# Where a weight matrix is split into two parts: on ScalarE and VectorE, or in two transfers of the POOL queue

## The chip, the cores and the metric

The kernel runs on one core of a Trainium2 chip. The metric is the device time of one launch in microseconds; the kernel before took 1216.84 us (median of 2 runs, 1215.64 to 1218.04). The engines are named as in the profile: PE is TensorE (matmuls; PEld is its loading of weights), DVE is VectorE, ACT is ScalarE, POOL is GpSimd, SP is the engine that only issues transfers. A transfer is issued on the queue of an engine, here SP's or POOL's, and each queue is worked through in order.

## The reference

One inference step of a one-layer decoder: 1024 prompt positions and 8 single-token decode sequences, width 1024. Four recurrent mixers (S5, SSD, HGRN2, GLA), all fed by one input projection, are followed by an output projection and an MLP. What matters here is the MLP:

```python
hn = rmsnorm(x, p['norm_mlp_g'])
x = x + jnp.square(jax.nn.relu(hn @ p['w_up'])) @ p['w_down']
```

`w_up` is 1024 x 4096 and `w_down` 4096 x 1024, all in float32. The other outputs are the recurrent states.

## The kernel before

The 1032 positions are worked on as two halves of the sequence, 512 columns (`hf` = 0) and 520 columns (`hf` = 1, in two chunks of 260). The channels lie on the 128 partitions.

**Products in two parts.** A float32 operand is held as the sum of two float32r tiles, a high part and a low part. `split` (line 213) makes them: ScalarE rounds the float32 tile into `hi` (`act`, line 157), VectorE subtracts `hi` from it into `lo` (`tt`, line 169). `mm3` (line 256) then issues three matmuls for each block of 128 x 128 weights: hi with hi, hi with lo, lo with hi, in that order. All matmuls go through line 199.

**Weights.** `wprep` (line 240) fetches one tile of 128 x 1024 weights in two halves of 512 columns: SP loads `raw` (line 249), and `split` makes `hi` and `lo`. Below, such a half of 256 KB is called a half weight. The buffers are `W_BUFS = 3, 4, 4` for `raw`, `hi` and `lo` (line 100); the projections and the MLP share them. A buffer is free again when the last instruction that reads it is done.

**Order.** `main` (line 1697) runs the input projection of both halves, the output projection and MLP of the first, then those of the second. `drive` (line 300) puts the mixers' work, two strands of their own, between the main products by estimated times. The order of the instructions on each engine and queue comes from a planner (line 1888) that simulates the program: an instruction is placed when the planner expects its operands to be there, lower priority numbers first. `wprep` runs 1000000 ahead of the rest (`Prio`).

**The MLP** (`mlp`, line 1454) has 8 blocks `fb` of 512 hidden channels. For each block of the first half it makes four products with `w_up` (`f` = 0 to 3, `product`, line 471, 8 blocks of weights each), squares the ReLU (`up`, line 1419) into four tiles `a`, and makes four products with `w_dn` (`q` = 0 to 3), each for two output blocks `n2` over the four `f`. For q = 0 the order of (n2, f) is written out at line 1489: n2 = 0 with f 0 to 2, n2 = 1 with f 0 to 2, then both with f = 3; column block `n2 * 4 + f` of the weights is used, so n2 = 0 reads the first half weight and n2 = 1 the second. Results are collected into `Y` (`collect`, line 1433).

In the second half of the sequence, block 0 runs in the same way. Blocks 1 to 7 make their up-projection in `fast_up` (line 1575) with seven products in place of eight; its weights come from `pair_weights` (line 1537), which loads `raw` on the POOL queue (line 1551) into buffers of another pool, `late`. `fast_up` also begins the down-projection of q = 0 (line 1624). Block 7 fetches its four `w_dn` tiles with `wprep` (line 1620).

**What else POOL issues.** In the output projection it stores the residual, `xd`, once for each of 8 output blocks and each half (line 1389); in the input projection it stores the projected channels (line 538).

Of the kernel before, what the change touches and what calls it, by code (L numbers as in the profile page):

```python
# [10 lines left out]
F32R = mybir.dt.float32r  # L11
I32 = mybir.dt.int32
AF = mybir.ActivationFunctionType
OP = mybir.AluOpType
# [85 lines left out]
W_BUFS = 3, 4, 4  # L100
# [7 lines left out]
class Kern:  # L108
# [131 lines left out]
    def wprep(self, src, off=-1000000, pool=None, pin=False):  # L240

        parts = []
        with Prio(self.tc, off):
            p, nr, nh, nl = (pool,) + L_BUFS if pool else (self.wp,) + W_BUFS
            for c in (slice(0, 512), slice(512, 1024)):
                raw = p.tile([128, 512], F32, tag='raw', name=self.n('raw'), bufs=nr)
                hi = p.tile([128, 512], F32R, tag='hi', name=self.n('hi'), bufs=nh)
                lo = p.tile([128, 512], F32R, tag='lo', name=self.n('lo'), bufs=nl)
                d = self.nc.sync.dma_start(raw, src[:, c])
                if pin:  # L250
                    self.tc.keep_in_program_order(d)
                self.split(hi, lo, raw)
                parts.append((hi, lo))
        return lambda k: (t[:, k % 4 * 128:k % 4 * 128 + 128] for t in parts[k // 4])

# [1198 lines left out]
    def mlp(self, hf, H2, ssq):  # L1454


        for fb in range(8):
            if hf and fb:
                A, first = yield from self.fast_up(fb, H2, R1 if fb == 7 else None)
            else:  # L1460
                A, first = [], None
                for f in range(4):
                    wt = self.wprep(self.I['w_up'][fb * 4 + f])
                    A.append(self.hidden())
                    ps = yield from self.product(hf, wt, H2)
                    if not hf and fb == f == 1:
                        R = self.inverse_squares(hf, ssq)
                    with self.first():
                        self.up(A[f], ps, hf)
                    if hf and f < 3:  # L1470
                        self.finish(8 + f)
                    if hf and f == 3:
                        ps = [self.px() for _ in CK[hf]]
                        self.sum_rows(hf, ps, ssq, True, True)
                        R1, R = self.row_factors(hf, ps), self.rows('R')
                        self.tt(R, R1, R1)
            if hf and fb == 7:
                break
            if fb == 0:
                Y = self.fp.tile([128, 8, WM], F32, tag='Y', name=self.n('Y'), bufs=1)  # L1480
                if hf:
                    self.differences(H2)
            for q in range(4):
                if q == 0 and first:
                    pp = first
                else:
                    wt, pp = self.wprep(self.I['w_dn'][fb, q]), self.pp(hf)

                    for n2, f0, f1 in ((0, 0, 3), (1, 0, 3), (0, 3, 4), (1, 3, 4)) if q == 0 else ((0, 0, 4), (1, 0, 4)):
                        yield from self.down(hf, wt, A, pp, n2, range(f0, f1))  # L1490
                with self.first():
                    for n2 in range(2):
                        self.collect(Y, q * 2 + n2, self.pieces(hf, pp[n2]), fb == 0)
                if hf and fb == 6:
                    for n2 in range(2):
                        self.residual(hf, Y, q * 2 + n2, R)
        if hf:
            yield from self.close(A, Y, self.sp.tile([128, WM], F32, tag='ssq', name=self.n('ssq'), bufs=1), first)
        else:
            self.final = Y, R, self.sp.tile([128, 512], F32, tag='nw', name=self.n('fsq'), bufs=1)  # L1500
# [74 lines left out]
    def fast_up(self, fb, H2, R):  # L1575

        h, A = 260, [self.hidden() for _ in range(4)]
        U = {}

        def step(pr, i):  # L1580
            if (pr, 'W') not in U:
                U[pr, 'W'] = self.pair_weights(fb, pr)
                U[pr, 'al'], U[pr, 'be'], U[pr, 'ga'] = self.pm()[:, :h], self.pm()[:, :h], self.px()[:, :h]
            al, be, ga = (U[pr, n] for n in ('al', 'be', 'ga'))
            bank, a, b = {1: (al, 'A11', 'B11'), 6: (be, 's2', 't2'), 7: (ga, 's3', 't3'), 2: (al, 'A12', 'B21'),
                              5: (be, 's1', 't1'), 3: (be, 's4', 'B22'), 4: (ga, 'A22', 't4')}[i]
            yield from self.seventh(U[pr, 'W'], H2, bank, a, b, i in (1, 6, 7))
            u = lambda n: self.late.tile([128, h], F32, tag=n, name=self.n(n), bufs=2)

            def out(f, c, x, bk, sign):  # L1590
                r = self.sp.tile([128, WM], F32, tag='io', name=self.n('r'), bufs=4)[:, :h]
                c0, c1 = c * h, c * h + h
                self.tt(r, bk, x, OP.add)
                if R:
                    self.stt(r, r, 0.0, R[:, c0:c1], OP.max if sign > 0 else OP.min, OP.mult)
                else:
                    self.act(r, r, AF.Relu, scale=float(sign))
                self.squares(A[f], c0, c1, r)
            f = 2 * pr
            with self.first():  # L1600
                if i == 1:
                    U[pr, 1] = u('u1')
                    self.act(U[pr, 1], al)
                elif i == 6:
                    U[pr, 2] = u('u2')
                    self.tt(U[pr, 2], be, U[pr, 1], OP.add)
                elif i == 2:
                    self.up(A[f], [(al, 0, h)], 1, R)
                elif i == 5:
                    u4 = u('u4')  # L1610
                    self.tt(u4, be, U[pr, 1], OP.add)
                    out(f + 1, 1, u4, ga, -1)
                elif i == 3:
                    out(f, 1, U[pr, 1], be, 1)
                elif i == 4:
                    out(f + 1, 0, U[pr, 2], ga, -1)
        for pr, i in ((0, 1), (0, 6), (0, 7), (0, 2), (0, 5), (1, 1), (0, 3), (1, 6), (0, 4), (1, 7), (1, 2), (1, 5)):
            yield from step(pr, i)
        if fb == 7:
            W = [self.wprep(self.I['w_dn'][7, q], pool=self.late if q > 1 else None, pin=True) for q in range(4)]  # L1620
            pp = [self.pm()[:, :h] for _ in range(2)]
            part = lambda n2, f: self.last_down(W, A, pp[n2], n2, (f,), 1)
        else:
            wt, pp = self.wprep(self.I['w_dn'][fb, 0]), self.pp(1)
            part = lambda n2, f: self.down(1, wt, A, pp, n2, (f,))
        yield from part(0, 0)
        yield from part(0, 1)
        yield from step(1, 3)
        yield from step(1, 4)
        for n2, f in ((1, 0), (1, 1), (0, 2), (1, 2), (0, 3), (1, 3)):  # L1630
            yield from part(n2, f)
        return A, (W, pp) if fb == 7 else pp
# [259 lines left out]
```

## Time and profile before

| | us |
|---|---|
| median of 2 runs | 1216.84 |
| profiled execution | 1216.4 |
| its span, first to last instruction | 1214.6 |
| PE busy | 1192.8 |
| DVE busy | 905.5 |
| ACT busy | 621.4 |
| POOL busy | 96.2 |

In the profile a group of instructions is named by its line, its engine and its tiles, out<-in; buffer numbers are left out. Where a helper issues an operation, the line is that of the helper. "Landing" of a transfer is counted from its issue. In a table by stage, each engine has its busy time and the number of its instructions, then follow the granted clock of PE, the busy share of the 16 DMA engines, and GB/s. In the list of waits stand the total, the number of times and the longest.

### The profile page before, as it was taken

To read this page: it belongs to the slowest core of one execution; us is meant where nothing else is said; L and a number is where in the kernel's file an instruction comes from. 1 tells how busy PE (TensorE), PEld (TensorE's weight loads), DVE (VectorE), ACT (ScalarE), POOL (GpSimd) and SP (SyncE) were. 2 spreads that over 40 slices of the span, in tenths; PEclk is the share of its full clock that TensorE was granted. 3 is DMA by queue.
4 is the path that set the end of the run, shared out by engine and by line. 5 is a ranking of instruction groups with operands and counts; after the bars stand their busy time and mean duration, and the time that the engine had idled before them with its cause. 6 is when DMAs were issued, how large, how long until landed. Compare 5 with 4: busy or idle time off the path is not lost. (4 is left out here: it accounts for less than half of the span.)

```text
span 1214.6 us, 23758 instructions
## 1 busy us (share of the span) xinstructions
PE 1192.8 (98%) x9107; PEld 1047.9 (86%) x9107; DVE 905.5 (75%) x2011; ACT 621.4 (51%) x1128; POOL 96.2 (8%) x159
## 2 busy tenths in 40 slices
PE   7999999999999999999999999999999999999996
PEld 4778888999988877887778787899999999999996
DVE  7997769787578589667658856496877776776896
ACT  6363353477364562555246633545675654554555
POOL 1113130000000100000000000001000100110000
PEclk9999999999999999999999999999999999999998
DMA  5564364365445352243224334356643233233432
GB/s 189 176 188 141 117 199 142 106 212 180 139 140 168 119 164 71 82 148 123 86 72 153 111 107 139 113 180 208 215 142 109 82 113 102 80 100 103 123 96 71
DMA packets 86049, 161.28 MB, mean 133 GB/s; under 512 B 13408, under 2 KB 19200, under 8 KB 85680
## 3 DMA queue, kind: packets, MB, share of 16 engines
q1 hardware_dynamic: 75952, 128.72, 33.9%
q0 software_dynamic: 9984, 31.05, 7.6%
q8 instruction: 72, 1.18, 0.4%
q14 instruction: 41, 0.34, 0.1%
HBM read 134.57 MB, written 25.16 MB: 132 GB/s over the span
## 5 line engine op out<-in xcount | busy, mean ns | idle before, releaser
L157 ACT ACTIVATE hi<-raw 128x512 fp32r<-128x512 f32 x362 | 223.7, 628 | 418.2 <-PE pm L199 327.0
L169 DVE TENSOR_TENSOR lo<-raw,hi 128x512 fp32r<-128x512 f32 x362 | 247.2, 688 | 83.4 <-ACT hi L157 82.2
L199 PE MATMUL pm<-a,hi 128*128 128x260 f32 (+1 forms) x1088 | 273.6, 338 | 0.4 <-ACT a L157 0.4
L199 PE MATMUL pm<-h,hi 128*128 128x512 f32 (+1 forms) x976 | 246.9, 344 | 0.2 <-DVE u L169 0.2
L199 PEld LDWEIGHTS pm<-a,hi 128*128 128x128 f32 x1088 | 182.8, 188 | 23.1 <-ACT a L157 0.8
L199 PEld LDWEIGHTS pm<-h,hi 128*128 128x128 f32 x976 | 164.7, 188 | 24.3 <-issue 2.0
L199 PE MATMUL pm<-a,lo 128*128 128x260 f32 (+1 forms) x544 | 171.1, 336 | 0.0
L199 PE MATMUL pm<-h,lo 128*128 128x512 f32 (+1 forms) x488 | 162.0, 343 | 0.0
L199 PE MATMUL pm<-xA,hi 128*128 128x512 f32 x352 | 114.9, 404 | 2.1 <-ACT hi L157 1.2
L199 PE MATMUL pm<-xB,hi 128*128 128x260 f32 x704 | 116.9, 287 | 0.0
L199 PEld LDWEIGHTS pm<-a,lo 128*128 128x128 f32 x544 | 97.6, 188 | 11.3 <-issue 0.3
L169 DVE TENSOR_TENSOR Y<-pm,Y 128x260 f32<-128x260 f32 (+1 forms) x120 | 63.8, 547 | 50.6 <-PE pm L199 49.9
L199 PEld LDWEIGHTS pm<-xB,hi 128*128 128x128 f32 x704 | 96.9, 188 | 3.9 <-issue 2.6
L199 PEld LDWEIGHTS pm<-h,lo 128*128 128x128 f32 x488 | 89.6, 188 | 11.4 <-issue 0.5
L199 PE MATMUL px<-a,hi 128*128 128x260 f32 x448 | 83.6, 282 | 0.0
L199 PEld LDWEIGHTS pm<-xA,hi 128*128 128x128 f32 x352 | 66.0, 190 | 20.1 <-ACT hi L157 3.9
L199 PE MATMUL pm<-xB,lo 128*128 128x260 f32 x352 | 72.4, 285 | 0.0
L199 PE MATMUL pm<-xA,lo 128*128 128x512 f32 x176 | 71.3, 405 | 0.0
L199 PEld LDWEIGHTS px<-a,hi 128*128 128x128 f32 x448 | 66.8, 188 | 0.0
L169 DVE TENSOR_TENSOR a<-r,a 128x260 fp32r<-128x260 f32 (+1 forms) x96 | 49.0, 514 | 9.1 <-ACT a L157 8.4
L199 PEld LDWEIGHTS pm<-xB,lo 128*128 128x128 f32 x352 | 54.5, 188 | 0.5
L1551 POOL DMA_DIRECT2D raw<-in_w_up_dram x56 | 30.0, 538 | 283.6 <-DVE lo L169 176.4
(435 smaller groups left out, 2030.5 us busy)
## 6 DMA issues: line engine op xcount, KB each, us to landing
raw<-in_w_dn_dram SPq DMA_DIRECT2D x128, 256.0 KB, 2.7
raw<-in_w_in_dram SPq DMA_DIRECT2D x88, 256.0 KB, 3.0
raw<-in_w_up_dram SPq DMA_DIRECT2D x72, 256.0 KB, 2.8
raw<-in_w_up_dram POOLq DMA_DIRECT2D x56, 256.0 KB, 3.0
raw<-in_w_out_dram SPq DMA_DIRECT2D x32, 256.0 KB, 3.2
x<-in_xT_dram SPq DMA_DIRECT2D x16, 260.0 KB, 3.3
x<-in_xT_dram SPq DMA_DIRECT2D x16, 256.0 KB, 3.7
xd<-x POOLq DMA_DIRECT2D x8, 260.0 KB, 3.3
```

Of the source, the lines that this page charges most:

```text
L157: return self.nc.scalar.activation(out, in_, f, **k)
L169: return self.nc.vector.tensor_tensor(out, a, b_, op)
L199: i = self.nc.tensor.matmul(out, l, r, start=start, stop=stop, **k)
L1551: self.nc.gpsimd.dma_start(x, self.I['w_up'][fb * 4 + 2 * pr + f][:, 512 * c:512 * c + 512])
```

## The change

A new function `wsplit` makes the two parts of the MLP's weights. It calls SP and VectorE no more. For each half weight POOL issues a load that converts float32 to float32r on its way into `hi`; ScalarE writes -1 times `hi` into `lo`; POOL issues a second load of the same weights that is added to `lo` as it lands. `raw` is not used there. It takes the place of `wprep` for `w_up` in `mlp` and for `w_dn` in `mlp` and in blocks 1 to 6 of `fast_up`. The input and output projections, `pair_weights` and the last block of the second half stay as they were. The numbers of buffers are the same.

```diff
+    def wsplit(self, src, off=-1000000):
+        parts = []
+        with Prio(self.tc, off):
+            for c in (slice(0, 512), slice(512, 1024)):
+                hi = self.wp.tile([128, 512], F32R, tag='hi', name=self.n('hi'), bufs=W_BUFS[1])
+                lo = self.wp.tile([128, 512], F32R, tag='lo', name=self.n('lo'), bufs=W_BUFS[2])
+                self.nc.gpsimd.dma_start(hi, src[:, c])
+                self.act(lo, hi, AF.Copy, scale=-1.0)
+                self.nc.gpsimd.dma_start(lo, src[:, c], accum_op=OP.add)
+                parts.append((hi, lo))
+        return lambda k: (t[:, k % 4 * 128:k % 4 * 128 + 128] for t in parts[k // 4])
...
-                    wt = self.wprep(self.I['w_up'][fb * 4 + f])
+                    wt = self.wsplit(self.I['w_up'][fb * 4 + f])
...
-                    wt, pp = self.wprep(self.I['w_dn'][fb, q]), self.pp(hf)
+                    wt, pp = self.wsplit(self.I['w_dn'][fb, q]), self.pp(hf)
...
-            wt, pp = self.wprep(self.I['w_dn'][fb, 0]), self.pp(1)
+            wt, pp = self.wsplit(self.I['w_dn'][fb, 0]), self.pp(1)
```

## The prediction

> **What bounds the kernel now.** I read the page first, then busy time by stage, then who waited for whom, then the groups and transfers that the change touches.
>
> ```profile
> span 1214.6 us, 23758 instructions
> PE 1192.8 (98%) x9107; PEld 1047.9 (86%) x9107; DVE 905.5 (75%) x2011; ACT 621.4 (51%) x1128; POOL 96.2 (8%) x159
> ```
>
> TensorE is busy for 98% of the span, VectorE for 75%, ScalarE for 51%. All idle time of TensorE together is 1214.6 - 1192.8 = 21.8 us. The page gives shares over the whole span, so I cut it by stage: the MLP of the first half (383 to 803 us), the output projection of the second half, the first MLP block of the second half, and its next six blocks.
>
> ```profile
> core 0: us, PE busy (x) PEld busy (x) DVE busy (x) ACT busy (x) POOL busy (x), PEclk, DMA share, GB/s
> 383.00:803.00 420.00, 417.70 (x2691) 331.73 (x2690) 291.09 (x592) 197.52 (x339) 7.79 (x5) 1.00 0.36 114
> 803.00:850.00 47.00, 47.00 (x396) 46.91 (x395) 34.70 (x62) 24.50 (x39) 5.92 (x11) 1.00 0.66 213
> 850.00:898.00 48.00, 48.00 (x394) 47.40 (x393) 39.20 (x76) 34.82 (x81) 2.15 (x4) 1.00 0.63 204
> 898.00:1160.00 262.00, 261.77 (x2177) 260.87 (x2176) 194.48 (x401) 137.45 (x294) 25.68 (x48) 1.00 0.33 104
> ```
>
> In the three stages whose weights change, TensorE idles 420.00 - 417.70 = 2.3, 0 and 0.23 us, at a granted clock of 1.00. A busy row could still hide a slow TensorE, so I look at the pace of its matmuls in the timeline and at the number of matmuls with a low part.
>
> ```profile
> 487.18 0.62 PE L199 MATMUL pm<-a,hi 128*128 128x512 f32 x2
> 487.87 0.62 PE L199 MATMUL pm<-a,hi 128*128 128x512 f32 x2
> 1068.09 2.87 PE px L199 x24
> 383.00:803.00 420.00, 202.43 (x512) 96.15 (x512) 87.14 (x128) 1.00 0.36 114
> ```
>
> The first two rows are one triple (hi, hi, lo) apart: 0.69 us for three matmuls of 512 columns, 0.23 each. The third is 24 matmuls of 260 columns in 2.87 us, 0.12 each. The last counts instructions with a low part between 383 and 803 us: 512 matmuls, and 128 on VectorE, so 128 half weights of four column blocks. A half is 12 matmuls there, 12 x 0.2315 = 2.78 us, and all are 128 x 2.78 = 355.6 of the 420 us; the rest is the mixers' small matmuls, put between. So a half comes due every 2.78 us where TensorE does nothing else, every 420 / 128 = 3.28 us on average, and every 24 x 0.12 = 2.88 us in the second half of the sequence. TensorE runs without gaps at its pace: it is the bound, and only a late operand can change the time.
>
> **What goes.**
>
> ```profile
> raw<-in_w_dn_dram SPq DMA_DIRECT2D x128, 256.0 KB, 2.7
> raw<-in_w_up_dram SPq DMA_DIRECT2D x72, 256.0 KB, 2.8
> L157 ACT ACTIVATE hi<-raw 128x512 fp32r<-128x512 f32 x362 | 223.7, 628 | 418.2 <-PE pm L199 327.0
> L169 DVE TENSOR_TENSOR lo<-raw,hi 128x512 fp32r<-128x512 f32 x362 | 247.2, 688 | 83.4 <-ACT hi L157 82.2
> ```
>
> 72 + 120 = 192 half weights take the new path: all of `w_up` that the SP queue loads, and `w_dn` without the 8 halves of the last block. VectorE loses 192 x 0.688 = 132 us. ScalarE swaps a rounding copy for a negating one of the same size, 0.63 us, so nothing. SP loses 192 issues. TensorE waits for VectorE almost nowhere (the 2.3 us above are its whole idle time in the long stage), so the gain is at most 2.3 + 0.23 = 2.5 us. I take 0.
>
> **What moves into the turnaround of a buffer.** `raw`, `hi` and `lo` have 3, 4 and 4 buffers. Before, the transfer filled a `raw` buffer ahead of time; once TensorE released a `hi` buffer, only a copy and a subtraction (0.63 + 0.69 us) stood between that and the next half. The first group shows it: ScalarE idled 327.0 us in front of this copy, waiting for TensorE's release. After, both transfers, one behind the other, and the copy lie between release and next use. The terms:
>
> ```profile
> raw<-in_w_up_dram POOLq DMA_DIRECT2D x56, 256.0 KB, 3.0
> raw<-in_w_out_dram SPq DMA_DIRECT2D x32, 256.0 KB, 3.2
> E<-cd SPq DMA_DIRECT2D x2, 1024.0 KB, 4.8
> q1 hardware_dynamic: 75952, 128.72, 33.9%
> L1551 POOL DMA_DIRECT2D raw<-in_w_up_dram x56: 537/537/544, 845.1 to 1161.4; - x56
> DMA to landing us min/median/max: 2.5/3.0/5.7
> ```
>
> Engines' share first: q1 moved 128.72 MB in 33.9% of 1214.6 us, 3.2 us per MB, so 0.84 us of all 16 engines per 0.262 MB half. One more transfer for each of 128 halves adds 128 x 0.84 / 420 = 0.26 to the share of 0.36: 0.62, about that of the output projection (0.66), whose loads land in 3.2 us where `w_dn` takes 2.7. So 0.5 us more than in a quiet stage.
>
> - Converted load: no row shows one. Bounds 2.5 and 5.7 us, the ends of the plain POOL load of the same size. I take its median and the contention, 3.0 + 0.5 = 3.5.
> - Negating copy: 0.63.
> - Adding transfer: no row shows one either. It reads the destination besides the source, so I treat it as one more 256 KB: from 2.7 us for 256 KB to 4.8 for 1 MB is 0.7 per 256 KB, so 3.5 + 0.7 = 4.2. Bounds again 2.5 and 5.7.
> - Hand-overs: release to POOL, landing to ScalarE, copy to POOL, each with what is queued ahead. POOL issues for 0.54 us and ScalarE is about half busy with instructions of 0.4 to 0.7. I take 3 x 0.4 = 1.2; bounds 0.3 and 2.5.
>
> Together 3.5 + 0.63 + 4.2 + 1.2 = 9.5 us (bounds 5.9 and 14.5).
>
> The Trainium skill ("Collectives: The Full Stack", section on the bandwidth ceiling) says that an add in the DMA path costs nothing itself, but reads two sources, and halves the rate. By it the adding transfer takes 0.84 us of the engines more than a plain one, so 4.3 instead of my 4.2, and the sum would rise by about 3 us; no row here shows it.
>
> **What the turnaround may last.** With four buffers, half n+4 is loaded once n is finished and is due when n+3 is finished: three halves, plus two matmuls, since the low part comes third. In the first half that is 3 x 2.78 + 0.46 = 8.8 us, and with mixers' work between (420 / 355.6 = 1.18) 10.3. The tightest place is in each `w_dn` block: at q = 0 the order is (n2 0, f 0 to 2), (1, 0 to 2), (0, 3), (1, 3), so both halves are released at the end, the first only 3 matmuls (0.69) before it, and the first half of q = 2 is due one product (5.56) later: 0.69 + 5.56 + 0.46 = 6.7, with mixers' work 7.9. In the second half the same sums are 3 x 2.88 + 0.48 = 9.1 and 0.72 + 5.76 + 0.48 = 7.0, and no strands are left to stretch them.
>
> With 9.5 us:
> - first half, q = 2: 8 blocks x (9.5 - 7.9) = 13 us;
> - first half, elsewhere: none where mixers' work lies between; where none does, 9.5 - 8.8 = 0.7 per round of four halves. I take half of the 128 halves: 64 / 4 x 0.7 = 11;
> - second half, first block: 2.5 at q = 2, and 12 / 4 x 0.4 = 1.2 for the rest: 4;
> - second half, six blocks: its up-projection there uses buffers of its own and gives time to refill, so once per block 9.5 - 7.0 = 2.5: 15.
>
> Sum +43 us. The profiled execution took 1216.4 us (span 1214.6 and 1.8 around it), the median of the runs is 1216.84. 1216.4 + 43 = **1259 us**. With the lower bounds (5.9) nothing stalls: 1216, or 1214 with the 2.5 gained. With the upper (14.5): (14.5 - 10.3) x 128 / 4 = 134 in the long stage and 8 x 2.4 = 19 more at its q = 2, 16 + 8 in the first block after, 6 x 7.5 = 45 in the rest: 222, about 1438.
>
> **What stands behind the new waits.** POOL's queue now holds, in one order, loads that wait for TensorE, adding transfers that wait for ScalarE, 16 stores of the residual and the 56 `raw` loads of the fast blocks. ScalarE's copy now waits for a landing, and behind it stand the ReLU, the squares and PSUM's evacuation.
>
> ```profile
> ACT hi L157 <- PE pm L199: 328.4, 172, 7.6
> 844.40 0.54 POOL L1389 DMA_DIRECT2D xd<-x  x1 [5.16 <-DVE x L169]
> 845.06 2.14 POOL L1551 DMA_DIRECT2D raw<-in_w_up_dram  x4
> 850.10 0.55 POOL L1389 DMA_DIRECT2D xd<-x  x1 [2.90 <-DVE x L169]
> ```
>
> ScalarE already stood up to 7.6 us at this place, so the order there tolerates such a wait: 0. On POOL, the rows show four loads put between two stores that each wait for VectorE: the planner places each instruction by when it expects it ready, not by program order. At 3.28 us per half the next load is expected (3.28 after its predecessor) before the adding transfer of the earlier one (3.5 + 0.63 = 4.1 after its own load), so I expect loads ahead of adding transfers, and no cost.
>
> **Rivals.**
> 1. *The cover holds* (not slower). If the transfers land as plain ones do, 3.0 + 3.7, and hand-overs take 0.6, the turnaround is 7.9. Only the six last blocks are then late, 6 x 0.9 = 5: 1222 us. For it: 8.8 or more of cover nearly everywhere, and 2.5 us landings exist. Against it: it needs no contention at nearly twice the traffic. It decides below about 8.5 us.
> 2. *POOL's order serialises* load, copy, adding transfer, next load: 3.0 + 0.3 + 0.63 + 0.3 + 0.54 = 4.8 us per half against 3.28 and 2.88. 128 x 1.52 + 16 x 1.92 = 226: 1442 us. It decides if the planner puts an adding transfer ahead of the next load. Against it: the rows above.
> 3. *The transfers are much slower*, turnaround 13: (13 - 10.3) x 32 = 86 and 19 more at q = 2, 18 in the first block, 36 in the others: 1376 us. For it: landings up to 5.7 us exist among plain loads already; no row bounds an adding one.
> 4. *Faster*, VectorE's 132 us reaching TensorE. The 2.5 us above speak against it: 1214 us at best.
>
> **How the numbers follow.** Forecast 0.45, rival 1 0.28, rival 2 0.10, rival 3 0.15, something that gains over 2% 0.02. The range leaves out rival 2, the top of rival 3 and the lowest few per cent: 1218 to 1395. A change under 2% (24 us) is what I count as none: faster 0.02, same 0.28, slower 0.45 + 0.10 + 0.15 = 0.70.
>
> **What would show it.** TensorE's idle time appears in the MLP stages alone, before matmuls on the first blocks of a half, released by the adding transfer into `lo`; most regular at q = 2, once per block. Landings on the POOL queue near 3.5 (load) and 4.2 us (add), DMA share near 0.6 between 383 and 840 us, VectorE down by about 132 us. Rival 1 shows as those landings with TensorE still full; rival 2 as POOL idle on ScalarE between each pair, loads following adding transfers one by one; rival 3 as adding transfers of 6 us and more. I am wrong in kind if TensorE waits for something else, a late ReLU or PSUM bank above all.

## The result and the profile after

The changed kernel takes 1408.41 us (median of 2 runs, 1403.55 to 1413.27) against 1216.84: 1.157 times the time before, interval 1.154 to 1.161. The prediction had the sign; its time was 149 us too low, and its range ended 13 us below the result.

First lines of the page of the changed kernel, and its group of negating copies:

```profile
span 1401.8 us, 23820 instructions
PE 1259.9 (90%) x9107; PEld 1078.6 (77%) x9107; DVE 793.1 (57%) x1819; ACT 616.9 (44%) x1127; POOL 368.5 (26%) x543
...
L157 ACT ACTIVATE lo<-hi 128x512 fp32r<-128x512 f32 x192 | 120.9, 630 | 456.5 <-DMA hi<-in_w_dn_dram 256.6
```

TensorE's share fell from 98 to 90%, but it also became *busier*: 1259.9 against 1192.8 us for the same 9107 matmuls. So two things were lost, idle time and pace. VectorE's group of subtractions fell from 247.2 to 116.2 us and its whole busy time by 112, and none of that reached the end.

The loss by stage. The three stretches are the MLP of the first half (from the first matmul on `h` to the first on `mixB`), then the output projection and first MLP block of the second half, then everything from the first matmul on `TS` to the end (`TS` is what `fast_up` multiplies; its blocks 1 to 6, whose `w_dn` takes the new path, are called the fast blocks below). Busy time by stage of the kernel before (the columns are those of the prediction's table: span, then PE, PEld, DVE, ACT, POOL, granted clock, share of the DMA engines, GB/s):

```profile
383.10:803.30 420.20, 417.90 (x2691) 331.90 (x2690) 291.29 (x592) 197.49 (x340) 7.79 (x5) 1.00 0.36 114
803.30:898.20 94.90, 94.90 (x787) 94.29 (x786) 73.61 (x137) 59.49 (x120) 8.07 (x15) 1.00 0.64 208
898.20:1214.60 316.40, 305.89 (x2518) 302.64 (x2516) 236.05 (x492) 167.19 (x360) 26.21 (x49) 0.99 0.31 98
```

The same stages of the changed kernel:

```profile
383.70:914.80 531.10, 455.94 (x2681) 340.98 (x2680) 218.68 (x470) 194.94 (x340) 185.72 (x256) 0.96 0.72 154
914.80:1034.00 119.20, 105.27 (x798) 101.97 (x797) 64.80 (x121) 60.28 (x121) 34.96 (x53) 0.94 0.75 197
1034.00:1401.80 367.80, 325.06 (x2517) 316.59 (x2516) 206.99 (x442) 165.67 (x356) 90.21 (x139) 0.94 0.49 119
```

The stages took 111, 24 and 51 us more, 186 of the span's 187. In the first, TensorE's idle time rose from 2.3 to 75.2 us, and its busy time by 38. The clock column gives the reason for about half of that 38: 0.04 x 531 = 21 us of full speed are missing; the other half stays open. Over the three stages it is 0.04 x 531 + 0.06 x 119 + 0.06 x 368, less 0.01 x 316 for the kernel before, about 47 us. That is the most it can be, since a slow clock costs nothing where TensorE stands idle; by the trace's clock records, 42 us when that time is left out.

The transfers of the changed kernel (issues with their number, size and median time to landing):

```profile
q0 software_dynamic: 65280, 131.74, 42.1%
hi<-in_w_dn_dram POOLq DMA_DIRECT2D x120, 256.0 KB, 4.2
lo<-in_w_dn_dram POOLq DMA_DIRECT2D x120, 256.0 KB, 4.6
hi<-in_w_up_dram POOLq DMA_DIRECT2D x72, 256.0 KB, 4.7
lo<-in_w_up_dram POOLq DMA_DIRECT2D x72, 256.0 KB, 4.6
```

And its list of waits:

```profile
POOL lo L266 <- ACT lo L157: 320.4, 127, 8.6
ACT lo L157 <- DMA hi<-in_w_dn_dram: 256.6, 76, 9.2
PE pm L199 <- DMA lo<-in_w_dn_dram: 43.1, 29, 4.7
PE pm L199 <- DMA lo<-in_w_up_dram: 39.9, 30, 4.1
...
PE pm L199 <- DMA hi<-in_w_dn_dram: 14.2, 12, 1.8
```

TensorE waits for the adding transfer, as predicted. But POOL stands 320 us in front of adding transfers whose copy has not been made, and what stands behind them in its queue stands with them. A stretch of POOL in the timeline of the changed kernel shows it:

```profile
557.32 1.42 POOL L264 DMA_DIRECT2D hi<-in_w_dn_dram  x2
563.27 0.87 POOL L266 DMA_DIRECT2D lo<-in_w_dn_dram  x1 [4.53 <-ACT lo L157]
563.82 0.86 POOL L264 DMA_DIRECT2D hi<-in_w_dn_dram  x1
564.35 1.22 POOL L266 DMA_DIRECT2D lo<-in_w_dn_dram  x1
```

The load at 563.82 starts without a wait of its own, right after an adding transfer that stood for 4.53 us: its buffer had come free meanwhile.

The pace, in the timeline of TensorE (a wait of 2.34 us, and the matmuls after it):

```profile
460.42 0.80 PE L199 MATMUL pm<-h,lo 128*128 128x512 f32 x1 [2.34 <-DMA lo<-in_w_up_dram]
461.01 1.05 PE L199 MATMUL pm<-h,hi 128*128 128x512 f32 x2
462.29 1.05 PE L199 MATMUL pm<-h,hi 128*128 128x512 f32 x2
466.37 0.62 PE L199 MATMUL pm<-h,hi 128*128 128x512 f32 x2
467.07 0.63 PE L199 MATMUL pm<-h,hi 128*128 128x512 f32 x2
```

From 461 a triple of matmuls comes every 1.28 us, from 466 again every 0.70, as before the change. Here the gap cost its own length and, over these 5.4 us, about 2.4 us of slow matmuls.

### The profile page after: what moved, and what is told of

Read it like the earlier page. It is cut to its first block, busy times and chain, and to the rows that moved or that the text cites. A ratio compares the mean times of both kernels' runs of the same rounds, so it can differ in the third digit from the quotient of the medians.

```text
span 1401.8 us, 23820 instructions
## 1 busy us (share of the span) xinstructions
PE 1259.9 (90%) x9107; PEld 1078.6 (77%) x9107; DVE 793.1 (57%) x1819; ACT 616.9 (44%) x1127; POOL 368.5 (26%) x543
## 3 DMA queue, kind: packets, MB, share of 16 engines
q0 software_dynamic: 65280, 131.74, 42.1%
## 4 chain that ended last, share of the span: by engine, by line
PE 19%; issue 19%; DMA 10%; POOL 10%; DVE 2%; ACT 2%; POOLq 0%; DVEq 0%; ACTq 0%
PE pm L199 15%; POOL lo L266 5%; POOL hi L264 4%; PE px L199 4%; DMA hi<-in_w_dn_dram 3%; DMA lo<-in_w_dn_dram 2%; DMA raw<-in_w_up_dram 2%; DMA hi<-in_w_up_dram 1%; DMA lo<-in_w_up_dram 1%; ACT lo L157 1%; DVE s L169 1%; DVE Y L169 0%; ACT hi L157 0%; DVE lo L169 0%; POOL raw L1565 0%
## 5 line engine op out<-in xcount | busy, mean ns | idle before, releaser
L157 ACT ACTIVATE lo<-hi 128x512 fp32r<-128x512 f32 x192 | 120.9, 630 | 456.5 <-DMA hi<-in_w_dn_dram 256.6
L199 PE MATMUL pm<-a,hi 128*128 128x260 f32 (+1 forms) x1088 | 286.9, 356 | 16.2 <-DMA hi<-in_w_dn_dram 14.2
L199 PEld LDWEIGHTS pm<-a,hi 128*128 128x128 f32 x1088 | 195.8, 203 | 44.4 <-DVE Y L169 10.7
L199 PE MATMUL pm<-a,lo 128*128 128x260 f32 (+1 forms) x544 | 180.5, 358 | 43.2 <-DMA lo<-in_w_dn_dram 43.1
L199 PE MATMUL pm<-h,lo 128*128 128x512 f32 (+1 forms) x488 | 171.5, 364 | 40.2 <-DMA lo<-in_w_up_dram 39.9
L157 ACT ACTIVATE hi<-raw 128x512 fp32r<-128x512 f32 x170 | 105.3, 625 | 152.9 <-PE pm L199 124.4
L266 POOL DMA_DIRECT2D lo<-in_w_dn_dram x120 | 106.3, 915 | 200.6 <-ACT lo L157 177.6
L169 DVE TENSOR_TENSOR lo<-raw,hi 128x512 fp32r<-128x512 f32 x170 | 116.2, 685 | 49.4 <-ACT hi L157 49.2
L266 POOL DMA_DIRECT2D lo<-in_w_up_dram x72 | 64.2, 900 | 162.7 <-ACT lo L157 142.8
L264 POOL DMA_DIRECT2D hi<-in_w_dn_dram x120 | 78.3, 685 | 101.7 <-PE pm L199 51.6
L169 DVE TENSOR_TENSOR r<-r 128x512 f32<-128x512 f32 x32 | 22.1, 691 | 136.4 <-ACT a L157 136.4
```

The lines of the kernel that those rows point to most:

```text
L157: return self.nc.scalar.activation(out, in_, f, **k)
L169: return self.nc.vector.tensor_tensor(out, a, b_, op)
L199: i = self.nc.tensor.matmul(out, l, r, start=start, stop=stop, **k)
L264: self.nc.gpsimd.dma_start(hi, src[:, c])
L266: self.nc.gpsimd.dma_start(lo, src[:, c], accum_op=OP.add)
```

## The experiments

Each is told as a difference from the changed kernel, unless it says otherwise; the kernel before took 1215.9 to 1217.5 us beside them (medians). A time marked "one run" was measured once.

### What each transfer costs

Only the converting load (VectorE subtracts, as before):

```diff
+                raw = self.wp.tile([128, 512], F32, tag='raw', ...)
                 self.nc.gpsimd.dma_start(hi, src[:, c])
+                self.nc.sync.dma_start(raw, src[:, c])
-                self.act(lo, hi, AF.Copy, scale=-1.0)
-                self.nc.gpsimd.dma_start(lo, src[:, c], accum_op=OP.add)
+                self.tt(lo, raw, hi.bitcast(F32), OP.subtract)
```

> Only the high part is made the new way: POOL loads with conversion into the high tile, SP loads raw beside it, VectorE subtracts as before the change. One transfer in the turnaround, 4.5 + 0.69 + about 1 = 6.2 us. Turnaround theory and POOL-order theory: no stalls, 1217 to 1225 us. Engine theory: one plain and one converting load per half, between 0.84 and 2.6 us of engine time saved nothing, 1330 to 1400 us.

1261.64 us (one run), above the 1217 to 1225 expected. Its transfers, then its first and third stage:

```profile
q0 software_dynamic: 37632, 81.39, 22.0%
hi<-in_w_dn_dram POOLq DMA_DIRECT2D x120, 256.0 KB, 3.3
```

```profile
383.90:812.40 428.50, 422.21 (x2692) 333.14 (x2691) 293.55 (x595) 127.64 (x216) 73.80 (x130) 1.00 0.64 190
914.10:1259.90 345.80, 317.14 (x2518) 313.49 (x2516) 243.19 (x500) 142.15 (x319) 49.71 (x93) 0.95 0.41 126
```

A converted load lands in 3.3 us, and in the long stage it costs 8 us in all. Yet the third stage loses 29, at a clock of 0.95. One block of it in the timeline, POOL's load and then TensorE:

```profile
1043.34 2.14 POOL L266 DMA_DIRECT2D hi<-in_w_dn_dram  x4 [4.82 <-PE px L199]
```

```profile
1046.44 0.73 PE L199 MATMUL pm<-a,hi 128*128 128x260 f32 x4 [2.56 <-DMA hi<-in_w_dn_dram]
```

All four halves of q = 2 and 3 are loaded together, the moment TensorE releases their buffers, and TensorE has nothing else to do. This is taken up below.

The converting load and a second transfer that overwrites instead of adding:

```diff
-                self.nc.gpsimd.dma_start(lo, src[:, c], accum_op=OP.add)
+                self.nc.gpsimd.dma_start(lo, src[:, c])
```

> The second transfer of each half weight overwrites the low tile with converted weights instead of adding to it, so the low part of the MLP's weights is left out of the result; chain, queues, copies and buffers are the same. It prices the reading of the destination. If the addition costs what one more 256 KB costs (0.7 us of landing), landing of the second transfer falls from 4.6 to about 3.9 us and the whole to about 1370 us; if the conversion and the contention are what costs, landings stay near 4.5 and the time near 1400 us; if the addition is the main cost, the second transfer lands in 3.0 us and the whole falls to about 1320 us.

1307.61 us (one run), 100 less than with the add and below all that was expected. Its transfers:

```profile
q0 software_dynamic: 65280, 131.74, 35.3%
hi<-in_w_dn_dram POOLq DMA_DIRECT2D x120, 256.0 KB, 3.3
lo<-in_w_dn_dram POOLq DMA_DIRECT2D x120, 256.0 KB, 3.3
```

The same bytes with the same instructions take 35.3% of 1305.8 us = 461 us of all engines, with the add 42.1% of 1401.8 = 590 (and in the serial order below 35.3% of 1674.9 = 591): 129 / 192 = 0.67 us more for each half. A converting load takes (22.0% of 1259.9 - 7.6% of 1214.6, the `raw` loads and stores that this queue had before) / 192 = 0.96 us. So an adding one takes 1.63, 1.7 times as much. For collectives, the Trainium skill ("Collectives: The Full Stack", section on the bandwidth ceiling) has an add read two sources where a copy reads one, at about half the rate; the trace agrees in direction, with 1.7 in place of 2. Landings, its own and those of the loads beside it, are 1 to 1.5 us longer.

Only the adding transfer (SP loads `raw`, ScalarE rounds it into `hi` and negates it, POOL adds):

```diff
+                raw = self.wp.tile([128, 512], F32, tag='raw', ...)
-                self.nc.gpsimd.dma_start(hi, src[:, c])
+                self.nc.sync.dma_start(raw, src[:, c])
+                self.act(hi, raw)
```

> Only the low part is made the new way: SP loads raw and ScalarE rounds it into the high part as before the change, then ScalarE writes the negative into the low tile and POOL adds. The first transfer is out of the buffer's turnaround, 0.63 + 0.63 + 4.6 + about 1.2 = 7.1 us. Turnaround theory: below 8.8 us everywhere but at q = 2, about 1220 to 1235 us. POOL-order theory: no loads stand on that queue, so the same 1220 to 1235. Engine theory: the bytes are the same, so about 1400 us.

1310.74 us (one run) against 1220 to 1235 expected. So one adding transfer in the turnaround, without any load in it, costs 95 us; it lands later here, 5.1 to 5.7 us:

```profile
lo<-in_w_dn_dram POOLq DMA_DIRECT2D x120, 256.0 KB, 5.7
lo<-in_w_up_dram POOLq DMA_DIRECT2D x72, 256.0 KB, 5.1
```

That turnaround is two copies, 5.1 to 5.7 and the hand-overs, 1.26 + 5.1 to 5.7 + 1.2 = 7.6 to 8.2 us: less than the 8.8 that the prediction had given as cover (the time from a buffer's release to its next use). So the cover, or the estimate of the hand-overs in it, was wrong too, and not only the transfers.

### A fifth buffer

```diff
+                self.half = getattr(self, 'half', -1) + 1
+                if self.half % 5 == 4:
+                    hi, lo = (self.wp.tile([128, 512], F32R, tag='raw', ...) for n in ('hi', 'lo'))
```

> Every fifth half weight of the MLP takes its high and low tile from the three raw buffers, which the MLP does not use after the change: five pairs of buffers instead of four, everything else as in the changed kernel. Turnaround theory (four buffers, and two landings of about 4.5 us with a copy, queues and hand-overs between release and next use, some 11.5 us together): one round of five halves is 11.5 + 2.8 us, 2.9 us per half, below the 3.28 us at which halves come due in the first half's MLP. That stage falls from 529 to about 440 us, the six later blocks from 322 to about 285, the whole to about 1280 us. POOL-order theory (a load is issued only behind the adding transfer of the half before the last, one queue): the order stays, so about 1400 us. Engine theory (load and addition occupy the 16 DMA engines for 2.6 us per half, and that sets the pace): the same bytes, about 1400 us.

1323.35 us, ratio 1.087 (1.084 to 1.090), between the expected 1280 and 1400: 85 us less than the changed kernel, from a buffer that changes no transfer. Its second and third stage take 105.1 and 334.7 us, its first 499.6: the time until a buffer is used again counts, but in the long stage 79 us stay. The planner also gave this kernel more loads ahead of adding transfers (at most 3 of the first 128 have none, against 37), so it doesn't tell buffers from POOL's order. The next pair does.

### POOL's order

In the first half of the changed kernel, POOL's order of instructions has one load ahead of the adding transfer for 81 of 128 halves, two or three for 10, and none for 37: there it is load, its adding transfer, next load. Two kernels hold the first half to one order with dependences that add no wait of another engine:

```diff
                 D.append((dh, dl))
                 if n < 128:
+                    if n > 1: self.after(dh, D[n - 2][1])
+                    if n: self.after(D[n - 1][1], dh)
```

> In the first half's 128 halves the POOL queue is held to one order: the load of half n+1, then the adding transfer of half n, then the load of n+2. The changed kernel's own POOL order has one load ahead of the adding transfer for 81 of them, none for 37 and two or three for 10. Queue theory (an adding transfer without a load ahead keeps the next load waiting through a landing, a copy and two hand-overs): following PE's and POOL's orders with landings of 4.6 us, the waits of the first half are 142 us in the changed kernel's order and 84 in this one; so 40 to 60 us less in that stage (529 to about 480) and about 1355 us in all. Buffer theory (only the turnaround of the four buffers counts, POOL's order does not): the stage stays within 10 us, 1398 to 1415 us in all.

1359.69 us, 1.1185 (1.114 to 1.123): 49 less, as the queue theory had it. The planner moved some of TensorE's matmuls too, but the cover of the 128 halves, counted along TensorE's order as below, was no longer than in the changed kernel (8.1 against 8.3 us on average), so POOL's order remains as the cause. Its first stage:

```profile
383.20:867.90 484.70, 442.37 (x2671) 332.77 (x2670) 217.72 (x467) 197.92 (x341) 184.64 (x255) 0.98 0.79 168
```

The other order, none ahead:

```diff
                 if n < 128:
+                    if n: self.after(dh, D[n - 1][1])
```

> The same 128 halves, with no load ahead of any adding transfer: load, copy, adding transfer, next load. Queue theory: each half takes at least the landing of its load, the copy, the two issues and the hand-overs, 3.3 to 4.6 + 0.63 + 0.9 + 0.55 + 0.7 = 6.1 to 7.4 us, so the stage takes 780 to 950 us instead of 529, and the kernel about 1660 to 1830 us. The prediction's second rival had priced this order at 4.8 us a half, 614 us for the stage and about 1490 in all. Buffer theory: no change, 1398 to 1415.

1676.71 us (one run). Its first stage:

```profile
382.40:1181.20 798.80, 544.15 (x2681) 392.12 (x2680) 223.65 (x474) 206.96 (x346) 187.76 (x258) 0.85 0.48 103
```

798.8 / 128 = 6.2 us for a half, as expected from landing, copy and issues one behind the other. The DMA engines are idle half of the time: the queue's order, not their throughput, sets this pace.

### Where four buffers come free at once

TensorE doesn't follow the order in which the code is written. Along its instructions in the kernel before and in the changed one, q = 0 and 1 of a fast block are interleaved, since the second needs the same `a` tiles; both then end together. In most of these blocks the four halves of q = 2 and 3 are due 1.5, 1.8, 2.0 and 8.7 us after their buffers are released in the trace of the kernel before; in the changed kernel q = 2 and 3 are interleaved as well, and it is about 1.7, 2.2, 2.5 and 2.1 us when stalls are left out and the pace is the full one. They are 24 of the 192 halves. Only these on the new path:

```diff
-                    wt = self.wsplit(self.I['w_up'][fb * 4 + f])
+                    wt = self.wprep(self.I['w_up'][fb * 4 + f])
...
-                    wt, pp = self.wsplit(self.I['w_dn'][fb, q]), self.pp(hf)
+                    wt, pp = (self.wsplit if hf and fb and q > 1 else self.wprep)(self.I['w_dn'][fb, q]), self.pp(hf)
```

> Only 24 of the 192 halves take the new path: those of w_dn at q = 2 and 3 in the six fast blocks of the second half; the other 168 are prepared as before the change. In the order that TensorE follows there, q = 0 and 1 are interleaved, their four buffers come free almost together, and the halves of q = 2 and 3 have 1.7 to 2.1 us until they are due. Buffer theory: landing 3.5, copy 0.63, adding transfer 4.2, hand-overs 1.2 less 1.7 of cover, and 2 us of slow matmuls after the gap: about 9.6 us in each of six blocks, 58 in all: 1265 to 1280 us. If the cost is spread evenly over the halves (engine time of the transfers): 24 / 192 x 192 = 24 us: 1235 to 1245 us.

1259.26 us, 1.034 (1.032 to 1.037): 43 us from an eighth of the halves. Less than the 58 expected, nearly twice what an even spread would give. All of it lies in the third stage, at a clock of 0.96:

```profile
897.10:1252.50 355.40, 318.88 (x2518) 311.37 (x2516) 222.83 (x468) 169.39 (x359) 60.28 (x97) 0.96 0.39 105
```

The complement, all but these:

```diff
-                    wt, pp = self.wsplit(self.I['w_dn'][fb, q]), self.pp(hf)
+                    wt, pp = (self.wprep if hf and fb and q > 1 else self.wsplit)(self.I['w_dn'][fb, q]), self.pp(hf)
```

> The complement: 168 halves take the new path, the 24 halves of w_dn at q = 2 and 3 in the six fast blocks are prepared as before. Buffer theory: the stage of the fast blocks falls back from 322 us to within 10 of the 262 before, the rest of the changed kernel's loss stays: 1345 to 1360 us. If the cost is spread evenly over the halves: 24 us less, 1380 to 1390 us.

1364.16 us, 1.120 (1.118 to 1.123): 44 less than the changed kernel, a little above the 1345 to 1360 expected. 43.1 + (1364.16 - 1216.14) = 191.1, and the whole change cost 191.6: the two parts add up.

### The clock by itself

The kernel *before*, with no new transfer: in fast block fb, ScalarE makes the rounding copy of the first half of q = 2 fb more times, and the other three copies come behind it.

```diff
+                    i = self.act(hi, raw)
+                    for _ in range(more):   # fb, at q = 2
+                        i = self.act(hi, raw)
```

> The kernel before, with no new transfer anywhere. In each fast block fb = 1 to 6 of the second half, ScalarE's rounding copy of the first w_dn half of q = 2 is issued fb more times (0.63 us each) before the other three halves' copies, so TensorE's operand comes (1 + fb) x 0.63 + 0.3 us after its buffer is released, against 1.7 us of cover. Gaps of TensorE expected: 0, 0.5, 1.1, 1.75, 2.4 and 3.0 us, 8.7 in all. Without a clock effect: 1216 + 9 = 1225 us, granted clock 1.00 throughout, 0.12 us per 260-column matmul right after each gap. With the effect seen in the changed kernel (half pace for about 4 us after gaps of 1.5 us or more): 2 us more in the blocks 4, 5 and 6: about 1231 us, 0.24 us per matmul after those gaps and not after the shorter ones.

1228.35 us, 1.010 (1.006 to 1.013), 11.6 more than the kernel before. TensorE's gaps were 0.54, 0.35, 1.01, 1.68, 2.34 and 3.00 us, 8.9 in all (8.7 expected). The last two, and the first matmuls after them:

```profile
1108.16 0.75 PE L199 MATMUL pm<-a,hi 128*128 128x260 f32 x4 [2.34 <-ACT hi L157]
1154.60 0.74 PE L199 MATMUL pm<-a,hi 128*128 128x260 f32 x4 [3.00 <-ACT hi L157]
```

The granted clock (third column from the right) after the one and after the other:

```profile
1109.66:1111.16 1.50, 1.50 (x15) 1.50 (x14) 0.38 (x1) 0.00 (x0) 0.00 (x0) 1.00 0.64 203
1156.60:1157.60 1.00, 1.00 (x5) 0.73 (x5) 1.00 (x3) 0.00 (x0) 0.00 (x0) 0.50 0.69 233
1158.60:1159.60 1.00, 1.00 (x10) 1.00 (x10) 0.25 (x1) 0.00 (x0) 0.00 (x0) 0.96 0.72 266
```

So the slow pace follows a gap alone, without any load on the DMA engines beyond the usual. But the expected limit of 1.5 us was wrong: 1.68 and 2.34 us left the clock at 1.00, 3.00 us halved it for about 3.4 us, which is 1.7 us of matmuls lost. What decides is taken up in the last section.

### The `raw` loads among the new transfers

```diff
-                    self.nc.gpsimd.dma_start(x, self.I['w_up'][fb * 4 + 2 * pr + f]...)
+                    self.nc.sync.dma_start(x, self.I['w_up'][fb * 4 + 2 * pr + f]...)
```

> The changed kernel with the 56 raw w_up loads of the fast blocks on SP's queue instead of POOL's, where they stand among the loads into hi and the adding transfers. Queue theory for the fast blocks (they hold the adding path up): 3 to 6 us less in each of six blocks, 1370 to 1390 us. Buffer theory (there the release of all four buffers at once decides, and POOL waits for PE, not for its own order): within 8 us of the changed kernel, 1400 to 1416.

1395.30 us, 1.147 (1.142 to 1.152), 13 less than the changed kernel: between the two expectations. The stages decide. The third, where these loads are, takes 373.4 us instead of 367.8:

```profile
1018.30:1391.70 373.40, 327.60 (x2518) 318.62 (x2516) 211.47 (x448) 169.44 (x365) 65.24 (x92) 0.94 0.48 118
```

So with the 24 halves on the new path, taking these loads off POOL's queue gained nothing in the fast blocks. The second stage is 7 us shorter, where the first of these loads stand among adding transfers, and the first 8, where there are none of them; that stage, unedited, took 536.9 us in the complement above and 531.1 in the changed kernel, so 8 us there is within what it varies by.

One wait in the fast blocks the prediction did not have, and no edit here removes it alone. Once in each block TensorE stands before a matmul on `TS` until ScalarE has made the rounded copy of its up-projection weight, which the change left as it was:

```profile
PE pm L199 <- ACT hi L157: 11.0, 8, 2.0
```

Of these 11.0 us 9.8 lie in the six fast blocks of the changed kernel, against 0.2 in the kernel before. It is still 9.4 with these loads on SP, and 9.7 of the 13.7 us that the complement loses in its third stage (330.1 against 316.4); it is gone where the second transfer overwrites, and where only the 24 halves take the new path. So it goes with the adding transfers of q = 0 and 1. By what way they make these copies late (ScalarE's own waits, the `raw` loads behind them on POOL) was not separated.

### All three edits, and then without the add

The POOL order with one load ahead, the 24 halves as before the change, and the `raw` loads on SP, in one kernel (the three diffs above):

> The changed kernel with three of the edits at once: the first half's POOL order (one load ahead of each adding transfer), the 24 halves of q = 2 and 3 in the fast blocks as before the change, the fast blocks' raw w_up loads on SP. Alone they gave 49, 44 and 13 us. If they are causes of their own (the third hardly, since it acted on the waits that the second takes away): 1408 - 49 - 44 = 1315, within 1300 to 1325. If each only shifted the same wait: above 1335. What stays, about 100 us, is then the turnaround in the first half against its cover, with PE's slow clock after the gaps.

1311.68 us, 1.077 (1.075 to 1.079): 97 less than the changed kernel, against 49 + 44 + a few. The effects add up, so they are causes of their own, the third (4 us here) too small to tell. Stages:

```profile
382.20:864.90 482.70, 441.57 (x2672) 332.83 (x2670) 217.53 (x467) 198.26 (x341) 185.20 (x256) 0.98 0.79 169
984.40:1310.10 325.70, 306.94 (x2518) 303.29 (x2516) 222.85 (x471) 167.15 (x364) 31.39 (x44) 0.99 0.42 113
```

Then, in that kernel, the second transfer overwrites instead of adding:

```diff
-                dl = self.nc.gpsimd.dma_start(lo, src[:, c], accum_op=OP.add)
+                dl = self.nc.gpsimd.dma_start(lo, src[:, c])
```

> The same three edits, and the second transfer overwrites its buffer instead of adding to it: the low part of the MLP weights is left out, all else stays. By PE's and POOL's orders the first half's waits are 84 us with landings of 4.6 us, 40 with 4.0 and 11 with 3.3 and 3.2. If the adding transfer's length (and the load that lies behind it in the queue) is what remains: landings 3.2 to 3.5 us, and 1230 to 1250 us. If the remainder belongs to POOL's, ScalarE's and the buffers' hand-overs, whatever the transfer does: 1280 to 1315.

1270.41 us, 1.044 (1.040 to 1.048), between the two expectations. Stages:

```profile
383.70:840.60 456.90, 434.04 (x2671) 333.76 (x2670) 218.63 (x467) 198.74 (x341) 140.47 (x256) 0.98 0.64 178
950.80:1270.80 320.00, 306.05 (x2518) 302.96 (x2516) 223.46 (x471) 167.63 (x364) 23.25 (x44) 0.99 0.38 115
```

The add itself is worth 41 us here; with POOL's own order and the 24 halves it was worth 100. A reason that fits, but was not tested by itself: there a longer landing is waited for twice, by the copy and by the loads that stand behind the waiting adding transfer. 53 us are left, 37 of them in the first stage (456.9 - 420.2), with transfers of 3.3 to 3.5 us. Which of the hand-overs they belong to (POOL's issues, ScalarE's queue, the shorter cover) was not taken apart.

## Why the prediction was right or wrong

The loss of 192 us, taken off by the runs in this order: about 49 POOL's order in the first half, 44 the 24 halves at q = 2 and 3, 4 the `raw` loads and what the edits do together, 41 the adding transfer beyond an overwriting second one, 53 the rest of the two-transfer turnaround. In another order the shares would differ: the add alone was worth 100. The slow clock, 42 to 47 us, is spread over all of them and is no item beside them.

- **"It is the bound, and only a late operand can change the time"; gain at most 2.5 us.** Right. VectorE's subtractions took 131 us less (132 forecast) and nothing came of it.
- **Converted load 3.5, adding transfer 4.2.** Both too low: 4.2 to 4.7 and 4.6. The converting load alone was sized well, 3.3 in its own kernel. What failed is that the adding transfer was taken for "one more 256 KB" at 0.7 us; against a second transfer that overwrites it cost 1.3 to 1.5 us of landing, and it delays the loads beside it. But this alone is not the miss: with 4.7 + 0.63 + 4.6 + 1.2 = 11.1 us, the forecast's sum for the first half gives 32 x 0.8 + 8 x 3.2 = 51 the way its upper bound was summed, and 16 x 2.3 + 16 x 0.8 + 8 x 3.2 = 75 the way its 43 were, not 111.
- **The copy, 0.63, in ScalarE's place for the old one.** Right (630 ns in the page's group).
- **What the turnaround may last: 8.8 to 10.3 us in the first half.** Wrong. It was worked out from the order in which the code is written. Along TensorE's own order in the kernel before, the time between the release of a `hi` buffer and its next use is 9.1 us on average over those 128 halves by the trace, below 7 for 14 of them. In the changed kernel it is about 8.3 when stalls and the slow clock are taken out, below 7 for 37: an estimate, and rather too long, since the rise in busy time that the clock leaves open is still in it. The planner laid out the new program anew, and interleaved more. What this alone costs in the first half was not measured.
- **q = 2 in the second half, cover 7.0, 15 us.** Wrong in the cover: 1.7 to 2.5 us, and 44 us measured, for q = 2 and 3 together. The views of the profile leave buffer numbers out; it takes the lists of the engines' instructions to see it.
- **POOL: "loads ahead of adding transfers, and no cost".** Wrong for 37 of 128 halves, and worth 49 us. The quoted stores and loads of POOL showed that the planner reorders by expected times, not that it had the times right. Rival 2, the serial order, was the right mechanism in part; fully made, it costs 6.2 us a half and not 4.8, since the landing of the load is over 4 us there too.
- **The 56 `raw` loads behind the new waits: no cost.** No cost of theirs was measured in the fast blocks beyond what the stages vary by.
- **"The order there tolerates such a wait: 0"** for ScalarE. Not settled. TensorE did wait 9.8 us for ScalarE's copies of up-projection weights, in the six fast blocks, where it had waited 0.2; whether ScalarE's own waits made them late was not separated.
- **A stall costs its length.** Never said, but the sum rests on it. It failed by 42 to 47 us: after a window with much idle time TensorE runs at half pace for 3.41 us (last section).
- **The signs.** TensorE idle in the MLP alone, released by the adding transfer into `lo`: yes in the first half; in the fast blocks it is more often the converting load into `hi` (14.2 us in 12 waits of the whole run, 7 of them there) and ScalarE's copies, named above. DMA share near 0.6: it is 0.72 in the first stage.

So the direction, the bound and the place were right. The size failed in two steps, both about order: the cover taken from the written order (at q = 2 and 3 of the fast blocks 44 us for 15), and POOL's queue taken to cost nothing (49). Two terms were too small or missing, the add's landing (41) and the clock, which is spread over the others. 53 us of the two-transfer turnaround were not taken apart.

## What to carry to other kernels

Where a step is moved from a prefetch buffer into the time between a buffer's release and its next use, measure that time along the engine's real order of instructions in the trace, buffer by buffer, and look for places where several are released at once; an average hides them. On an in-order queue that mixes loads and steps which wait for another engine, count how many loads stand ahead of each waiting step: here 37 of 128 with none cost 49 us. And price a stall of TensorE at its length plus the slow matmuls after it, here 1.7 us for each 3.41 us at half pace.

## What the runs showed of the hardware

- **An add in the transfer** took 1.63 us of all 16 DMA engines for 256 KB, a converting load 0.96, the plain loads and stores of the same queue before 7.6% of 1214.6 us for 31.05 MB, or 0.78 for 256 KB. Landing: 3.0 plain; 3.1 to 3.5 converting, without adding transfers beside it, and 4.1 to 4.7 with them; 4.1 to 5.7 adding.
- **The clock.** In the changed kernel's trace the granted clock is full or half, and the times at which it changes lie whole multiples of 3.41 us apart. Cut into windows of that length, the record shows what decides: not the length of a gap, but TensorE's idle time within one window. Two windows, each with the one behind it (span, busy time of PE and the rest as above, the clock third from the right):

```profile
404.19:407.60 3.41, 1.53 (x7) 0.91 (x5) 3.41 (x9) 1.33 (x3) 2.67 (x4) 1.00 0.61 95
407.60:411.02 3.42, 2.90 (x15) 2.46 (x16) 2.84 (x17) 0.63 (x1) 1.09 (x2) 1.00 0.94 214
445.15:448.56 3.41, 1.35 (x5) 0.49 (x3) 0.00 (x0) 0.75 (x2) 1.03 (x2) 1.00 0.65 160
448.56:451.97 3.41, 3.13 (x7) 2.51 (x8) 0.70 (x1) 1.49 (x3) 0.94 (x2) 0.50 0.88 176
```

A gap of 2.40 us lies across the edge at 407.60 and leaves 3.41 - 1.53 = 1.88 us idle in the first window; the clock stays full. Of a gap of 1.48 us, 1.20 lie before the edge at 448.56; with shorter ones that window has 3.41 - 1.35 = 2.06 us idle, and the next one runs at half clock. From 383 us on, all 17 windows at full clock with 1.9 us or more of idle time were followed by one at half clock, four of nine between 1.7 and 1.9 us, and one of 175 with less. Over the 13 traces of the changed kernel and the experiments it is 143 of 143 with 2.0 us or more, 63 of 132 between 1.5 and 2.0, and 5 of 2268 below; what decides between 1.5 and 2.0 us stays open. In the run with gaps alone, the 2.34 us lay 1.65 and 0.68 on the two sides of an edge, and 2.75 of the 3.00 fell into one window. The Trainium skill ("TensorE: Matmul & The Clock Gate", Part 1, on the clock gate) has a free-running window of 3.4 us over which activity is judged; the trace agrees. Its section on why this matters advises against gaps over about 3 us; here some 1.9 us of idle time within one window were enough.
